# Centred gate sums as two rounded products, and a second pass that begins eight steps later, in a two-layer attention kernel

## The chip, the cores and the metric

The kernel runs on one core of one Trainium2 chip. The metric is the device time of one execution in microseconds (us), the median over several runs. Beside it stands one profiled execution, from which every row of a view is taken.

## The reference

Two layers over 2048 latent tokens and 256 context tokens, model width 1024. The even layer has two groups of heads side by side: softmax attention with latent projections, and gated linear attention in both directions (4 heads, key width 64, value width 128). The odd layer is a neighbourhood attention. The change touches the linear attention alone:

```python
def gla_inputs(gq, gk, gv, g_lr, gate_w, gate_b):
    ...
    logits = jnp.einsum('bnzr,zrk->bnzk', r, gate_w) + gate_b
    g = (jax.nn.log_sigmoid(logits.astype(jnp.float32)) / GATE_TAU).reshape(bsz, n, 2, B_HEADS, B_DK)
    return q, k, v, g[:, :, 0], g[:, :, 1]

def gla_scan(q, k, v, g, s0):
    ...
    def step(state, inp):
        qi, ki, vi, gi = inp
        b = jnp.cumsum(gi, axis=-2)
        b_last = b[..., -1:, :]
        q_t = qi * jnp.exp(b)
        k_t = ki * jnp.exp(-b)
        att = jnp.where(mask, jnp.einsum('bhld,bhmd->bhlm', q_t, k_t), 0.0)
        o = jnp.einsum('bhld,bhde->bhle', q_t, state) + jnp.einsum('bhlm,bhme->bhle', att, vi)
        k_dec = ki * jnp.exp(b_last - b)
        state = state * jnp.exp(b_last)[..., 0, :, None] + jnp.einsum('bhld,bhle->bhde', k_dec, vi)
        return state, o
    ...

def readout(a, b, za, zb):
    ...
    b = rms_norm(b, gla_gain).reshape(bsz, n, B_WIDTH).astype(zb.dtype) * jax.nn.silu(zb)
    return jnp.dot(jnp.concatenate([a, b], axis=-1), w_out)
```

## The kernel before, in words

The 2304 tokens are 18 tiles of 128. After the projections, `even_mix` runs the softmax attention (`even_attention`) and the linear attention (`gla`) at the same time. The program is written attention block by attention block, with the linear attention's code between them, and a scheduler of the framework sets each engine's order of instructions from a model of their times and from the order in which they are written. Places where the code asks that an instruction be issued after another (`issue_after`) bind it further.

The softmax attention goes through 4 pairs of heads, 5 query blocks each (one of the 256 context tokens, four of 512), and per block through its key tiles. A key tile has two score tiles `st`, one per head. Each is three products of rounded parts (high by high L1016, high by low L1017, low by high L1018), one exponential on ACT into `apt` (L106), and an accumulation on DVE (L1007); the value products (L958) follow some key tiles later, four key tiles at a time. Three PSUM banks hold score tiles, two hold the linear attention's results (`gl`). Counted over the whole attention there are 592 score tiles.

Products run on operands of full precision, which PE does in two records each, or on rounded operands (type `F32R`), one record each. A value split into a rounded part and the rounded remainder keeps nearly its whole precision; the kernel does that for its large matrix products.

The linear attention works on chunks of 128 tokens in three parts:

- First pass. `front(c)` makes the gate's logits (L728), their log-sigmoid through three ACT operations and one DVE operation (L734, tile `G`), and sums along the tokens, centred on the chunk's middle, as a product with a triangle `tri` of ones and minus ones: one product of 256 columns per direction (L739). Two exponentials of the result scale queries and keys. The first and last rows of `G` are written out (`gE`), since the scans need them. `back(c)` scales queries and keys (L761), transposes them (L768), makes the chunk's state increment (L773, L774), the products within the chunk for both directions (L782), their masks and the sum of both on DVE (L785, L787, tile `gat`), and the product with the values (L791). The chunks are staggered: a chunk's `back` is written between the steps of the next two chunks' `front`.
- Two scans over the 18 chunks, forward on GpSimd (POOL) and backward on DVE (`gsb`, L827 to L829).
- Second pass, one chunk at a time: `enter` adds the state's part (L848, L849) to what the first pass left, squares the sum on ACT and adds up the squares per head on DVE (L853), and takes the power on POOL; `leave` normalises, multiplies with the gate and transposes back. The results go to a buffer in memory, `RT`.

`even_attention` calls `hook` once per key tile, 296 times. From call 166 on every fourth call does one step of `later()`: six steps that load and split weights of the output projection, then the second pass, one chunk per step, with a further weight step in every second one, then the last weights. What is left of it when the last query block begins (call 278) is done there in one go. After the attention the output projection reads `RT`, its first two tiles' products being laid at the end of the attention.

Of the kernel before, what the change touches and what calls it, by code (L numbers as in the profile page):

```python
# [11 lines left out]
F32R = mybir.dt.float32r  # L12
AF = mybir.ActivationFunctionType
ALU = mybir.AluOpType
AX = mybir.AxisListType
PSUM = bass.MemoryType.PSUM

P = 128
# [70 lines left out]
class Kern:  # L89
# [600 lines left out]
    def gla(self, gp, gs, g1, gd, pp, tag):  # L690

        nc = self.nc
        g = nc.gpsimd
        H = 4
# [8 lines left out]
        nc.vector.tensor_tensor(out=gw[64:97], in0=raw[64:97], in1=gw[64:97], op=ALU.subtract)  # L703
        tri = self.tl(g1, [P, 4, P], "tri", bufs=1)
        nc.sync.dma_start(tri[:], self.i["tri"])
        gn = self.tl(gp, [P, 4], "gn")
        nc.sync.dma_start(gn[:], self.i["gla_norm"])
        g.tensor_scalar(out=gn[:], in0=gn[:], scalar1=0.5, scalar2=None, op0=ALU.mult)
# [6 lines left out]
        z4 = lambda a: a.rearrange("p (h z d) -> p h z d", z=2, h=H)  # L715

        def front(c):

            ps = bank()
            u3 = self.tl(gs, [P, 3, 32], "gu3")  # L720
            nc.sync.dma_start(u3[:], self.Un[c, :, 1024:1056].unsqueeze(1).to_broadcast([P, 3, 32]))
            nc.tensor.transpose(ps[:96, :P], u3[:].rearrange("p n d -> p (n d)"), self.ident[:])
            r = rT[c % 2]
            self.act(r[:96, :], ps[:96, :P])
            nc.vector.tensor_tensor(out=r[32:64, :], in0=ps[32:64, :P], in1=r[32:64, :], op=ALU.subtract)
            yield
            lg = bank()
            nc.tensor.matmul(lg[:], r[:], gw[:], start=True, stop=True)  # L728
            e = self.tl(gs, [P, 512], "ge")
            self.act(e[:], lg[:], AF.Abs)  # L730
            self.act(e[:], e[:], AF.Exp, scale=-1.0)
            self.act(e[:], e[:], AF.Ln, bias=1.0)
            G = self.tl(g1, [P, 512], "gG", bufs=1)
            nc.vector.scalar_tensor_tensor(out=G[:], in0=lg[:], scalar=0.0, in1=e[:], op0=ALU.min, op1=ALU.subtract)  # L734
            G4 = G[:].rearrange("p (h z d) -> p h z d", z=2, h=H)
            yield
            mid = bank()
            for z in range(2):
                nc.tensor.matmul(mid[:].rearrange("p (h z d) -> p h z d", z=2, h=H)[:, :, z, :], tri[:, z, :], G4[:, :, z, :], start=True, stop=True)  # L739
            nc.sync.dma_start(self.gE[c, :, 2], G[0::127])  # L740
            qt = self.tl(g1, [P, 512], "gqt", bufs=1)
            kt = self.tl(g1, [P, 512], "gkt", bufs=1)
            self.act(qt[:], mid[:], AF.Exp, scale=1 / 16)
            for z, t in enumerate((127, 0)):
                nc.sync.dma_start(self.gE[c, z : z + 1, 0], qt[t : t + 1])
            self.act(kt[:], mid[:], AF.Exp, scale=-1 / 16)
            nc.sync.dma_start(self.gE[c, :, 1], kt[0::127])
            tiles[c] = qt, kt
            yield
# [55 lines left out]

        tiles, inputs = {}, {}
        fr = [front(c) for c in range(NT)] + [iter(())] * 2
        fetch_u(0)
        for c in (0, 0, 1, 0, 1):
# [34 lines left out]
        def enter(c, qT, oi, zb):  # L844

            ps = bank()
            for h in range(H):
                nc.tensor.matmul(ps[:, h * P : h * P + P], qT[:, h, :], Dl[c][:, h, :], start=True, stop=True)  # L848
            nc.vector.tensor_tensor(out=oi[:], in0=ps[:], in1=oi[:], op=ALU.add)  # L849
            sq = self.tl(gs, [P, 512], "ge")  # L850
            self.act(sq[:], oi[:], AF.Square)
            ss = self.tl(gs, [P, H], "gss")
            nc.vector.tensor_reduce(out=ss[:], in_=sq[:].rearrange("p (h t) -> p h t", h=H), axis=AX.X, op=ALU.add)  # L853
            self.rpow(ss[:], ss[:], 1.0 / 128, EPS)
            return c, oi, zb, ss

# [13 lines left out]
        def second():  # L870

            order = self.back_order()
            old, cur = None, fetch(order[0])
            for c in order[1:] + [None, None]:
                if old:
                    leave(*old)
                old = enter(*cur) if cur else None
                cur = fetch(c) if c is not None else None
                yield
# [166 lines left out]
    def even_mix(self, e1, win, hT):  # L1046
        nc = self.nc
        self.RT = self.scr("RT", (KD, P, T), F32)
        self.x1 = self.scr("x1", (T, D), F32)
        with ExitStack() as es:  # L1050
            with ExitStack() as esa:
# [4 lines left out]
                g1 = self.pool(es, "glA", bufs=2, side="right", reuse_waits="tile")  # L1056
                esg = ExitStack()
                gp = self.pool(esg, "glC", side="right", reuse_waits="tile")
                gs = self.pool(esg, "glS", bufs=2, side="right", reuse_waits="tile")
                count, ld, w = [0], [], {}  # L1060

                def hook(mm, ex):

                    count[0] += 1
                    if count[0] >= 166 and count[0] % 4 == 2:
                        with self.tc.issue_after(mm.ins), self.tc.issue_after(ex.ins), self.tc.issue_after(self.add.ins):
                            next(slow, None)

# [22 lines left out]
                def later():  # L1091
# [11 lines left out]
                    for _ in ws:  # L1103
                        yield

                att = self.even_attention(ap, pp, hook)
                next(att)
                second, slow = self.gla(gp, gs, g1, gd, pp, "gl"), later()
# [773 lines left out]
```

## Time and profile before

| | us |
|---|---|
| median of 3 runs | 3619.09 |
| lowest and highest | 3616.67, 3619.68 |
| the profiled execution | 3617.2 |
| its span, from first to last instruction | 3615.4 |

The profile has a row per instruction of the engines PE (matrix products), PEld (their weight loads), DVE, ACT and POOL. The page sums up busy times; further views group them by line and shape, by stretch of time, or list who waited for whom. In a row of groups stand the count after an x, then the busy time in us, the mean duration in ns, and the idle time before with what ended it; in a row of waits the total in us, the number of times and the longest; in the timeline the start, the duration and the instruction, with the idle time in brackets. Since products are pipelined, PE's durations overlap: how long one takes is read from the distance of the starts. The times of the stages, by the first and last start of their lines: the softmax attention from 1085.1 to 1927.0 us, the centred sums from 1122.0 to 1543.5 us, the second pass's products with the state from 1646.9 to 1834.3 us.

### The profile page before, as it was taken

What the parts mean: (1) busy time and instruction counts of PE and PEld (TensorE: products, weight loads), DVE (VectorE), ACT (ScalarE), POOL (GpSimd) and SP (SyncE); (2) the same over time, 40 slices, a digit from 0 to 9 for tenths busy, and PEclk for the clock granted to TensorE, in tenths of its full rate; (3) what the DMA queues carried; (4) which work ended last, traced back from release to release, by engine and by line L of the source; (5) the groups of instructions that cost most, each with busy time, mean ns of one, the idle gap of its engine ahead of it and who ended that gap; (6) DMA issues with size and microseconds to landing.
All of it is one profiled execution on the core that took longest, in us unless ns stands there. A gap on an engine that the chain in (4) does not pass through costs nothing. (4 is left out here: it accounts for less than half of the span.)

```text
span 3615.4 us, 51630 instructions
## 1 busy us (share of the span) xinstructions
PE 3523.6 (97%) x18260; PEld 2734.3 (76%) x18260; DVE 2372.3 (66%) x4876; ACT 1430.5 (40%) x2705; POOL 1212.6 (34%) x1342
## 2 busy tenths in 40 slices
PE   8999999999999999999999999999999999999899
PEld 6988998888886666656667878888788886555577
DVE  4677665888886776787664345444587874667721
ACT  5544551111115555555653134444422223555510
POOL 1433430111011232212312233333334444677743
PEclk9999999999999999999999999999999999999999
DMA  7555463222233343334534544456643437888654
GB/s 253 149 153 159 141 191 99 87 77 84 75 109 89 83 104 83 94 92 129 163 91 143 162 164 127 145 143 199 212 139 123 139 122 202 213 213 222 185 178 146
DMA packets 396683, 513.62 MB, mean 142 GB/s; under 512 B 61229, under 2 KB 275197, under 8 KB 390522
## 3 DMA queue, kind: packets, MB, share of 16 engines
q1 hardware_dynamic: 353242, 418.68, 40.0%
q0 software_dynamic: 20192, 56.97, 5.6%
q10 hardware_dynamic: 22992, 34.68, 2.8%
q8 instruction: 145, 2.38, 0.3%
q14 instruction: 112, 0.92, 0.1%
HBM read 330.61 MB, written 179.59 MB: 141 GB/s over the span
## 5 line engine op out<-in xcount | busy, mean ns | idle before, releaser
L1007 DVE TENSOR_TENSOR acc<-acc,apt 128x512 f32<-128x512 f32 x512 | 376.4, 764 | 150.6 <-ACT apt L106 147.0
L666 DVE TENSOR_REDUCE mm<-mx 128x1 f32<-128x512 f32 (+1 forms) x656 | 392.7, 627 | 90.6 <-PE mx L665 82.3
L106 ACT ACTIVATE apt<-st 128x512 f32<-128x512 f32 (+1 forms) x592 | 342.9, 593 | 269.0 <-PE st L1018 229.5
L958 PE MATMUL av<-apt,av 128*64 128x512 f32 (+1 forms) x1184 | 269.2, 592 | 0.0
L1016 PE MATMUL st<-aq,akh 97*128 97x512 f32 x576 | 246.8, 428 | 0.2 <-ACT apt L106 0.2
L665 PE MATMUL mx<-mk,mq 96*128 96x512 f32 (+1 forms) x656 | 238.5, 372 | 0.0
L1017 PE MATMUL st<-aq,akh 96*128 96x512 f32 x576 | 229.1, 398 | 0.0
L1018 PE MATMUL st<-aq,akl 96*128 96x512 f32 x576 | 228.5, 397 | 0.0
L1450 DVE CUSTOM_DVE_ANT_1 mx<-mx,mtab 128x465 f32<-128x465 f32 (+14 forms) x576 | 183.9, 338 | 47.2 <-PE mx L1444 34.5
L106 ACT ACTIVATE u<-gm 128x352 f32<-128x352 f32 (+1 forms) x144 | 70.3, 495 | 358.5 <-PE gm L131 207.7
L106 ACT ACTIVATE opt<-opt 128x930 f32<-128x930 f32 (+9 forms) x144 | 119.2, 830 | 234.5 <-POOL opt L1748 137.0
L958 PEld LDWEIGHTS av<-apt,av 128*64 128x64 f32 x1184 | 79.9, 137 | 152.0 <-issue 150.0
L1708 DVE TENSOR_TENSOR opt<-st,tab 128x64 f32<-128x64 f32 (+10 forms) x576 | 143.0, 314 | 78.3 <-PE st L1548 44.7
L1583 POOL TENSOR_TENSOR oacc<-oacc,opt 128x682 f32<-128x682 f32 (+9 forms) x144 | 173.9, 1230 | 37.8 <-ACT opt L106 36.6
L1016 PEld LDWEIGHTS st<-aq,akh 97*128 97x128 f32 x576 | 109.0, 189 | 72.7 <-issue 44.2
L665 PEld LDWEIGHTS mx<-mk,mq 96*128 96x128 f32 x656 | 122.7, 188 | 11.7
L1018 PEld LDWEIGHTS st<-aq,akl 96*128 96x128 f32 x576 | 110.2, 191 | 25.5
L1017 PEld LDWEIGHTS st<-aq,akh 96*128 96x128 f32 x576 | 110.6, 192 | 17.8
L106 ACT ACTIVATE x<-px,modB,modA 128x128 f32<-128x128 f32 x272 | 99.1, 468 | 58.5 <-PE px L335 39.5
L1547 PE MATMUL st<-q,kt 128*128 128x480 f32 (+5 forms) x256 | 98.7, 388 | 20.2 <-DVE opt L1708 14.8
L129 PE MATMUL gm<-w0h,hhi 128*128 128x512 f32 x288 | 115.3, 400 | 2.3 <-DVE hhi L347 2.3
L129 PE MATMUL gm<-w1h,hhi 128*128 128x512 f32 x288 | 116.7, 405 | 0.0
(584 smaller groups left out, 9906.5 us busy)
## 6 DMA issues: line engine op xcount, KB each, us to landing
q<-Q SPq DMA_DIRECT2D x48, 512.0 KB
H<-x ACTq DMA_DIRECT2D x36, 512.0 KB
adaw<-ada_w SPq DMA_DIRECT2D x64, 256.0 KB
x<-H SPq DMA_DIRECT2D x32, 512.0 KB
K1t<-okt POOLq DMA_DIRECT2D x32, 512.0 KB, 6.7
kt<-K1t SPq DMA_DIRECT2D x32, 512.0 KB
mtab<-rpb_q SPq DMA_DIRECT2D x16, 899.0 KB
QT<-qkhl SPq DMA_DIRECT2D x36, 384.0 KB
```

Source lines behind the costliest of these rows:

```text
L106: return self.nc.scalar.activation(out, in_, func, **kw)
L129: self.nc.tensor.matmul(out, lh(k), rh(k), start=j == 0, stop=False)
L665: mm = nc.tensor.matmul(ps[:, :w], q[:A_QK, (t % 6) * P : (t % 6) * P + P], k[:A_QK, k0 : k0 + w], start=True, stop=True)
L666: nc.vector.tensor_reduce(out=m[:, t, n : n + 1], in_=ps[:, :w], axis=AX.X, op=ALU.max)
L958: nc.tensor.matmul(O[j, nb][i * 64 : i * 64 + 64, :w], V[j, kt // TT][:, kt % TT, i * 64 : i * 64 + 64], pts[i][:, :w], start=n == 0, stop ...
L1007: self.add = nc.vector.tensor_tensor(out=acc[i][:, :w], in0=a[:, :w], in1=pts[i][:, :w], op=ALU.add)
L1016: nc.tensor.matmul(ps[:, :w], kh[: A_QK + 1, i, kq], qh[: A_QK + 1, :w], start=True, stop=False)
L1017: nc.tensor.matmul(ps[:, :w], kh[:A_QK, i, kq], ql[:A_QK, :w], start=False, stop=False)
L1018: mm = nc.tensor.matmul(ps[:, :w], kl[:A_QK, i, kq], qh[:A_QK, :w], start=False, stop=True)
L1450: nc.vector.tensor_tensor_reduce(out=s, in0=s, in1=tb[:, ri : ri + rn, ci : ci + cn], scale=1.0, scalar=-3e38, op0=ALU.add, op1=ALU.max, a ...
L1583: self.psum = nc.gpsimd.tensor_tensor(out=a, in0=a, in1=pts[:, :, a0 - r0 : a1 - r0, :], op=ALU.add)
L1708: nc.vector.tensor_tensor(out=pt[:, d[0], d[1]], in0=ps[:, d[0], d[1]], in1=tabs[j][i][:, ri : ri + rn, ci : ci + cn], op=ALU.add)
```

## The change

The centred sums' product with full-precision operands becomes two with rounded ones. The log-sigmoid stays in the tile `e`; ACT copies it, rounding, into `G`; DVE makes the remainder `L` (in a further buffer of the small tiles `ge`); the triangle is rounded once into `trr`. Per direction PE then adds up the products of `trr` with `G` and with `L`. The rows for `gE` are now read from `e`. In the second pass the four heads' sums of squares are made by four DVE operations that multiply and add up in one, instead of an ACT square and a DVE sum. And `later()` begins at call 174 instead of 166.

```diff
+        trr = self.tl(gp, [P, 2, P], "trr", F32R, bufs=1)
+        self.act(trr[:], tri[:, :2, :])
...
-            G = self.tl(g1, [P, 512], "gG", bufs=1)
-            nc.vector.scalar_tensor_tensor(out=G[:], in0=lg[:], scalar=0.0, in1=e[:], op0=ALU.min, op1=ALU.subtract)
-            G4 = G[:].rearrange("p (h z d) -> p h z d", z=2, h=H)
+            nc.vector.scalar_tensor_tensor(out=e[:], in0=lg[:], scalar=0.0, in1=e[:], op0=ALU.min, op1=ALU.subtract)
+            nc.sync.dma_start(self.gE[c, :, 2], e[0::127])
+            G = self.tl(g1, [P, 512], "gG", F32R, bufs=1)
+            self.act(G[:], e[:])
+            L = self.tl(gs, [P, 512], "ge", F32R)
+            nc.vector.tensor_tensor(out=L[:], in0=e[:], in1=G[:], op=ALU.subtract)
+            G4, L4 = z4(G[:]), z4(L[:])
             yield
             mid = bank()
             for z in range(2):
-                nc.tensor.matmul(mid[:].rearrange("p (h z d) -> p h z d", z=2, h=H)[:, :, z, :], tri[:, z, :], G4[:, :, z, :], start=True, stop=True)
-            nc.sync.dma_start(self.gE[c, :, 2], G[0::127])
+                nc.tensor.matmul(z4(mid[:])[:, :, z, :], trr[:, z, :], G4[:, :, z, :], start=True, stop=False)
+                nc.tensor.matmul(z4(mid[:])[:, :, z, :], trr[:, z, :], L4[:, :, z, :], start=False, stop=True)
...
             sq = self.tl(gs, [P, 512], "ge")
-            self.act(sq[:], oi[:], AF.Square)
             ss = self.tl(gs, [P, H], "gss")
-            nc.vector.tensor_reduce(out=ss[:], in_=sq[:].rearrange("p (h t) -> p h t", h=H), axis=AX.X, op=ALU.add)
+            for h in range(H):
+                o = slice(h * P, h * P + P)
+                nc.vector.tensor_tensor_reduce(out=sq[:, o], in0=oi[:, o], in1=oi[:, o], scale=1.0, scalar=0.0,
+                                               op0=ALU.mult, op1=ALU.add, accum_out=ss[:, h : h + 1])
...
-                    if count[0] >= 166 and count[0] % 4 == 2:
+                    if count[0] >= 174 and count[0] % 4 == 2:
```

Line numbers of the changed kernel are higher by up to eight (L1016 is L1024, L791 is L797, L785 is L791 there). Each engine's order moves over the whole attention. Three places show how.

PE, the centred sums of the tenth chunk. Before (`st` score tiles, `av` value products, `gl` the linear attention's results):

```order
L958 MATMUL av_13576<-apt_13603,av_13417 64x512
L958 MATMUL av_13576<-apt_13609,av_13417 64x512
L739 MATMUL gl_11298<-gG_11251,tri_10547 128x4x64 x2
L782 MATMUL gl_11312<-gqT_11271,gkT_11272 128x128
L1016 MATMUL st_13649<-aq_13452,akh_1874_10509 128x512
L1017 MATMUL st_13649<-aq_13452,akh_1874_10509 128x512
```

and in the change:

```order
L1026 MATMUL st_13783<-aq_13544,akl_13507 128x512
L745 MATMUL gl_11349<-gG_11300,trr_10549 128x4x64
L746 MATMUL gl_11349<-ge_11302,trr_10549 128x4x64
L745 MATMUL gl_11349<-gG_11300,trr_10549 128x4x64
L746 MATMUL gl_11349<-ge_11302,trr_10549 128x4x64
L1024 MATMUL st_13789<-aq_13544,akh_1875_10510 128x512
```

Two products have become four, and they stand between other instructions of the attention than before.

PE, ahead of the tenth chunk's product with its values. Before, where four score tiles and six value products stand between the products within the chunk and the first row shown, and the product with the values (L791) follows the last one:

```order
L958 MATMUL av_13841<-apt_13799,av_12798 64x512
L958 MATMUL av_13841<-apt_13805,av_12798 64x512
L728 MATMUL gl_11403<-gw_10543,rT_1891_10553 128x512
L1016 MATMUL st_13846<-aq_13777,akh_1877_10512 128x512
L1017 MATMUL st_13846<-aq_13777,akh_1877_10512 128x512
L1018 MATMUL st_13846<-aq_13777,akl_13218 128x512
L1016 MATMUL st_13852<-aq_13777,akh_1877_10512 128x512
L1017 MATMUL st_13852<-aq_13777,akh_1877_10512 128x512
L1018 MATMUL st_13852<-aq_13777,akl_13218 128x512
L1016 MATMUL st_13860<-aq_13777,akh_1877_10512 128x512
L1017 MATMUL st_13860<-aq_13777,akh_1877_10512 128x512
L1018 MATMUL st_13860<-aq_13777,akl_13218 128x512
```

and in the change, where the first row shown ends the first score tile behind the products within the chunk:

```order
L1026 MATMUL st_13952<-aq_13869,akl_13310 128x512
L1024 MATMUL st_13958<-aq_13869,akh_1877_10512 128x512
L1025 MATMUL st_13958<-aq_13869,akh_1877_10512 128x512
L1026 MATMUL st_13958<-aq_13869,akl_13310 128x512
L1024 MATMUL st_13966<-aq_13869,akh_1874_10509 128x512
L1025 MATMUL st_13966<-aq_13869,akh_1874_10509 128x512
L1026 MATMUL st_13966<-aq_13869,akl_13405 128x512
L730 MATMUL gl_11460<-gw_10543,rT_1892_10555 128x512
L1024 MATMUL st_13972<-aq_13869,akh_1874_10509 128x512
L1025 MATMUL st_13972<-aq_13869,akh_1874_10509 128x512
L1026 MATMUL st_13972<-aq_13869,akl_13405 128x512
L797 MATMUL gl_11472<-gu_11316,gat_11445 128x128 x4
```

Seven score tiles, eight value products and the gate product ahead of the product with the values have become four score tiles and the gate product. So it is in the ninth to fourteenth chunk and in the sixteenth.

DVE, the masks (`ge`, `gat`) of the last chunk among the steps of the backward scan (`gsb`, `D`) and the normalisation of an attention block (`den`, `rc`). Before:

```order
L894 TENSOR_TENSOR den_14886<-den_14886,rc_14890 128x256
L828 TENSOR_TENSOR gsb_12096<-gsb_12096,D_1908_10572 64x512
L895 SCALAR_TENSOR_TENSOR rc_14890<-den_14886,rc_14890 128x256
L829 TENSOR_TENSOR D_1908_10572<-gsb_12092,fac_1926_10590 64x512
L896 TENSOR_TENSOR rc_14890<-av_14818,rc_14890 128x256
L785 TENSOR_TENSOR ge_11988<-gl_11990,tri_10547 128x512
L827 TENSOR_TENSOR gsb_12100<-gsb_12096,fac_1925_10589 64x512
L785 TENSOR_TENSOR gat_11987<-gl_11989,tri_10547 128x512
L828 TENSOR_TENSOR gsb_12100<-gsb_12100,D_1907_10571 64x512
L787 TENSOR_TENSOR gat_11987<-gat_11987,ge_11988 128x512
```

and in the change:

```order
L1015 TENSOR_TENSOR acc_3034_14841<-acc_3034_14841,apt_15022 128x512
L834 TENSOR_TENSOR gsb_12184<-gsb_12184,D_1910_10575 64x512
L1015 TENSOR_TENSOR acc_3033_14840<-acc_3033_14840,apt_15030 128x512
L1015 TENSOR_TENSOR acc_3034_14841<-acc_3034_14841,apt_15036 128x512
L835 TENSOR_TENSOR D_1910_10575<-gsb_12180,fac_1928_10593 64x512
L791 TENSOR_TENSOR ge_12080<-gl_12082,tri_10547 128x512
L791 TENSOR_TENSOR gat_12079<-gl_12081,tri_10547 128x512
L833 TENSOR_TENSOR gsb_12188<-gsb_12184,fac_1927_10592 64x512
L1015 TENSOR_TENSOR acc_3033_14840<-acc_3033_14840,apt_15044 128x512
L1015 TENSOR_TENSOR acc_3034_14841<-acc_3034_14841,apt_15050 128x512
L793 TENSOR_TENSOR gat_12079<-gat_12079,ge_12080 128x512
```

The normalisation and two scan steps no longer stand ahead of and between the masks; two accumulations stand behind them. On PE, four value products and four score tiles stood before between the last of these chunk's products and the one that needs `gat`; in the change eight and five.

## The prediction

> **What bounds the kernel now.** I read the page's totals first, then the busy time by stretch around the changed code, then who waited for whom there, then the timeline of the changed products.
>
> ```profile
> span 3615.4 us, 51630 instructions
> PE 3523.6 (97%) x18260; PEld 2734.3 (76%) x18260; DVE 2372.3 (66%) x4876; ACT 1430.5 (40%) x2705; POOL 1212.6 (34%) x1342
> ```
>
> ```profile
> core 0: us, PE busy (x) PEld busy (x) DVE busy (x) ACT busy (x) POOL busy (x), PEclk, DMA share, GB/s
> 1120.00:1550.00 430.00, 426.25 (x2197) 271.19 (x2197) 305.63 (x425) 243.55 (x468) 108.88 (x109) 1.00 0.36 90
> 1550.00:1645.00 95.00, 92.00 (x422) 54.84 (x420) 90.71 (x134) 50.99 (x88) 11.01 (x9) 1.00 0.25 73
> 1645.00:1840.00 195.00, 195.00 (x956) 122.97 (x954) 137.69 (x217) 117.73 (x249) 59.25 (x58) 1.00 0.53 148
> ```
>
> PE is busy 97% of the span. The three stretches are the first pass of the linear attention, its two scans, and its second pass, all laid between the products of the softmax attention. PE has work in all three, at a granted clock of 1.00; DVE is 71% busy in the first, 95% in the second and 71% in the third, ACT 57%, 54% and 60%. A busy row can hide stalls, so I look at PE's waits from 1120 to 1928 us:
>
> ```profile
> PE gl L791 <- DVE gat L787: 3.0, 1, 3.0
> PE gl L782 <- DVE rT L725: 2.2, 3, 0.7
> PE den L889 <- DVE rc L895: 0.7, 1, 0.7
> PE gl L768 <- DVE gG L734: 0.6, 1, 0.6
> PE st L1016 <- ACT apt L106: 0.2, 1, 0.2
> ```
>
> They come to 6.7 us in 808 us. So here a PE microsecond removed is a microsecond gained, and DVE or ACT time added costs nothing until it makes PE wait.
>
> **The centred sums.** Each of 18 chunks does two full-precision products with the triangle, 256 columns each. One chunk's pair between attention products, from PE's timeline:
>
> ```profile
> 1365.97 0.40 PE L1018 MATMUL st<-aq,akl 96*128 96x512 f32 x1
> 1366.21 1.03 PE L739 MATMUL gl<-gG,tri 128*128 128x256 f32 x4
> 1366.88 0.58 PE L1016 MATMUL st<-aq,akh 97*128 97x512 f32 x1
> 1367.30 0.40 PE L1017 MATMUL st<-aq,akh 96*128 96x512 f32 x1
> 1367.54 0.40 PE L1018 MATMUL st<-aq,akl 96*128 96x512 f32 x1
> ```
>
> The durations overlap; the starts count. Rounded products of 512 columns follow one another every 0.235 us. From the start of L739 to that of L1017 are 1.09 us; less one such step for L1016, the pair costs 0.86 us, or 0.215 for each of its four records. What a rounded product of 256 columns costs is seen in the later neighbourhood attention, on PE and on PE's weight loads:
>
> ```profile
> 2700.05 0.40 PE L129 MATMUL gm<-w0h,hhi 128*128 128x512 f32 x1
> 2700.28 0.40 PE L1437 MATMUL mx<-mk,mz 128*128 128x256 f32 x2
> 2700.52 0.39 PE L130 MATMUL gm<-w0l,hhi 128*128 128x512 f32 x1
> 2700.05 0.42 PEld L1437 LDWEIGHTS mx<-mk,mz 128*128 128x128 f32 x2
> ```
>
> Two of them take 0.24 us start to start, 0.12 each, each with a weight load of its own. Four per chunk are 0.48. Saved: 0.86 - 0.48 = 0.38 us a chunk, times 18 = **6.9 us**, all on the path that sets the end. The bounds are 0.12 and today's 0.215 a product (nothing saved); I take 0.12, the row of the same width, kind and full weight load.
>
> [...]
>
> **What the first pass pays for it** is an ACT copy (rounding) and a DVE subtraction per chunk. Means by shape:
>
> ```profile
> L1007 DVE TENSOR_TENSOR acc<-acc,apt 128x512 f32<-128x512 f32 x512 | 376.4, 764 | 150.6 <-ACT apt L106 147.0
> L787 DVE TENSOR_TENSOR gat<-gat,ge 128x512 f32<-128x512 f32 x18 | 14.8, 823 | 0.0
> L785 DVE TENSOR_TENSOR ge<-gl,tri 128x512 f32<-128x512 f32 x18 | 12.4, 689 | 0.5
> L853 DVE TENSOR_REDUCE gss<-ge 128x4 f32<-128x512 f32 x18 | 12.2, 679 | 1.0 <-ACT ge L106 0.9
> L106 ACT ACTIVATE D<-wraw 128x512 fp32r<-128x512 f32 x9 | 5.6, 622 | 0.0
> L106 ACT ACTIVATE ge<-goi 128x512 f32<-128x512 f32 x18 | 11.2, 621 | 0.0
> ```
>
> The copy is like the split of a weight, 0.62 us; the subtraction lies between 0.69 and 0.82. That is 11 us more for ACT and at most 15 for DVE over 430 us in which they idle 186 and 124: counted as nothing. The order shows why the chain itself is covered: between the score tile of the last exponential ahead of the copy and the second product PE has at least five score tiles, 5 x 3 x 0.235 = 3.5 us, and in all but one chunk also eight or more value products. Behind the waiting copy on ACT stand the exponentials that free PE's three score banks; that is the last rival. The boundary rows now leave by DMA from the unrounded tile; on SP that DMA keeps its place, between the writes of a chunk's own outputs and of its queries, so nothing new waits there. The one rounding of the triangle stands behind the gate weights' rounding and before the first products: nothing.
>
> **The order around it** moves by more than that. The last chunk held PE for the 3.0 us shown above. DVE's timeline, and PE's product that waited:
>
> ```profile
> 1569.09 0.68 DVE L785 TENSOR_TENSOR ge<-gl,tri 128x512 f32<-128x512 f32 x1
> 1569.80 0.74 DVE L827 TENSOR_TENSOR gsb<-gsb,fac 64x512 f32<-64x512 f32 x1
> 1570.57 0.69 DVE L785 TENSOR_TENSOR gat<-gl,tri 128x512 f32<-128x512 f32 x1
> 1571.29 0.69 DVE L828 TENSOR_TENSOR gsb<-gsb,D 64x512 f32<-64x512 f32 x1
> 1572.01 0.69 DVE L787 TENSOR_TENSOR gat<-gat,ge 128x512 f32<-128x512 f32 x1
> 1564.91 1.94 PE L958 MATMUL av<-apt,av 128*64 128x512 f32 x8
> 1566.77 0.50 PE L1016 MATMUL st<-aq,akh 97*128 97x512 f32 x1
> 1572.85 0.57 PE L791 MATMUL gl<-gu,gat 128*128 128x128 f32 x3 [3.00 <-DVE gat L787]
> ```
>
> The masks were late because DVE had scan steps and a normalisation ahead of and between them. Eight value records, four products, took 1.86 us. Before, PE had four value products and four score tiles (4 x 0.705) ahead of the waiting product, 4.7 us; now eight and five, 7.2 us. Were DVE as late as before, the wait would fall from 3.0 to 0.5: **2.5 us gained** (bounds 0 and 3.0).
>
> In seven other chunks (the ninth to fourteenth and the sixteenth) the order now leaves PE only four score tiles and the gate product, 4 x 0.705 + 0.235 = 3.05 us, where DVE must do two masks and their sum, 0.69 + 0.69 + 0.82 = 2.2 us. The 0.85 between them must hold the hand-overs and what DVE still has in hand. I charge 0.15 each, **1.0 us lost**; the bounds are nothing and one accumulation late each, 7 x 0.76 = 5.3.
>
> **The second pass.** ACT loses its square (0.62), DVE its sum (0.68), for four multiply-and-sum operations of 128 elements, each with a read of its sum. The nearest are the masked maxima of 124 elements, whose start-to-start distances are 0.25 and 0.38 us:
>
> ```profile
> 2705.95 0.33 DVE L1450 CUSTOM_DVE_ANT_1 mx<-mx,mtab 128x124 f32<-128x124 f32 x1
> 2706.20 0.26 DVE L1450 CUSTOM_DVE_ANT_1 mx<-mx,mtab 128x56 f32<-128x56 f32 x1
> 2708.35 0.30 DVE L1450 CUSTOM_DVE_ANT_1 mx<-mx,mtab 128x124 f32<-128x124 f32 x1
> 2708.73 0.39 DVE L1450 CUSTOM_DVE_ANT_1 mx<-mx,mtab 128x217 f32<-128x217 f32 x1
> ```
>
> Four cost 1.0 to 1.5 us, 0.3 to 0.8 more than the sum did: 6 to 15 us of DVE over a stretch of 195 us in which it idles 57. Nothing reaches PE. L787 and L1007, with both inputs in SBUF, are slower on average (0.82, 0.76) than L785, which reads PSUM (0.69). [...]
>
> The eight steps' delay moves the second pass, its DMAs on SP and the six first weight splits by 16 score tiles. In the order its last transpose stands at tile 543 of 592 instead of 527, so 49 tiles remain; the last weights are still split, and the first output tiles still loaded, before the attention's last products. The same PE work lies elsewhere between the same attention products: nothing, unless its cover, attention still to run, were gone. Beyond the stage the order differs only in a few exchanged products: nothing.
>
> **The sum** is made against the profiled execution, 3617.2 us (span 3615.4 and 1.8 around it): -6.9 - 2.5 + 1.0 = -8.4, so 3608.8. The median of the three runs is 3619.1, 1.9 higher; from it the same change gives **3610.7 us**. A measurement of this kernel tells about 0.2% (7.2 us) from no change, so the line lies at 3611.9 and the forecast only just beyond it.
>
> **Rivals.** *The narrow places.* DVE is one accumulation late at each of the seven, +5.3, and the last chunk still waits: 3619.1 - 6.9 + 5.3 = 3617.5; with the last chunk relieved 3615. For it: DVE is 71% busy, its accumulations take 0.76 where 0.69 is possible. Against: PE waited for that operation once in 18 chunks. Chance 0.15, no change.
>
> *Short products don't hide their weight loads,* or the strided columns, or the second product, aren't done at 0.12 us, so that the change doesn't do what it says. The loads of the triangle today:
>
> ```profile
> L739 PEld LDWEIGHTS gl<-gG,tri x72: 187/188/193, 1121.8 to 1543.3; 128*128 128x128 f32 x72
> L739 PE MATMUL gl<-gG,tri x72: 377/378/483, 1122.0 to 1543.5; 128*128 128x256 f32 x72
> ```
>
> The number of loads stays at 72. If each product lasts its load's 0.19 us, the saving is (0.86 - 0.76) x 18 = 1.8; at 0.215 it is 0. With -2.5 and +1.0 the time is 3615.8 to 3617.6. Against: the L1437 pair. Chance 0.09, no change.
>
> *Slower: the rounding copy holds up ACT.* It waits for the log-sigmoid on DVE, with up to three exponentials between in the order, none in one chunk. If DVE starts it three accumulations late, 3 x 0.69 = 2.07, and takes 0.69 for it, ACT stands 2.76 us; PE's two free score banks cover 2 x 0.705 = 1.41; 1.35 is lost, times 18 = 24 us: 3619.1 - 6.9 + 24 = 3636. It decides from 1.41 + 14.1/18 = 2.2 us of standing on, where it outweighs the gain by 7.2. For it: the new hand-over goes ACT, DVE, ACT, DVE. Against: PE waited for ACT's exponentials 0.2 us in all. Chance 0.10.
>
> **How the numbers follow.** The forecast has 0.66: by the bounds of its terms 0.54 lies below 3611.9 and 0.12 above. With the two middle rivals, 0.15 + 0.09, no change has 0.36; slower has 0.10. The low end takes the whole 3.0 us wait and the other 3.7 us of PE's waits as gone: 3619.1 - 6.9 - 3.0 - 3.7 = 3605.5. The high end, 3619, takes in both middle rivals. Left out are the slower case and a little below.
>
> **What would show it.** Right: two rounded rows in place of L739's, together 72 records at steps of 0.12 us; PE's wait for the last masked sum under 1 us; DVE higher in the second pass with PE's waits unchanged. Wrong: steps of 0.19 or more at the new products; PE waiting for the masked sums in the later chunks; score products waiting for exponentials while ACT stands at the rounding copy.

## The result, and the profile after

The changed kernel takes 3612.4 us (median of 14 runs, 3606.4 to 3617.5); the kernel before, run beside it on the same chip, 3620.1 us. The ratio is 0.9981, with a 95% interval from 0.9973 to 0.9989: faster by 0.11 to 0.27%. The profiled execution's span went from 3615.4 to 3608.2 us, by 7.2.

After's page totals, then its busy times in the same three stretches:

```profile
span 3608.2 us, 51577 instructions
PE 3515.8 (97%) x18260; PEld 2726.7 (76%) x18260; DVE 2394.8 (66%) x5020; ACT 1431.6 (40%) x2706; POOL 1210.2 (34%) x1342
...
1120.00:1550.00 430.00, 425.29 (x2212) 269.86 (x2211) 321.60 (x447) 252.03 (x489) 108.69 (x112) 1.00 0.37 90
1550.00:1645.00 95.00, 94.51 (x426) 55.55 (x427) 87.81 (x128) 49.16 (x85) 8.03 (x6) 1.00 0.25 70
1645.00:1840.00 195.00, 195.00 (x949) 122.25 (x949) 144.84 (x337) 112.78 (x231) 57.42 (x55) 1.00 0.55 151
```

PE is as full as before and its number of records is the same; DVE has 16.0 us more in the first stretch (third busy column, 321.6 against 305.6) and 7.2 more in the third. PE's busy time is 1.0 us lower in the first (425.3 against 426.3) and the same in the third. What PE waited for from 1120 to 1928 us:

```profile
PE gl L797 <- DVE gat L793: 3.0, 6, 0.9
PE den L897 <- DVE rc L903: 1.4, 1, 1.4
PE gl L730 <- DVE ge L791: 0.4, 1, 0.4
PE st L1024 <- ACT apt L106: 0.4, 2, 0.2
```

They are 5.2 us instead of 6.7. The wait for the masked sum (L797 for `gat`) has the same 3.0 us as before, but in six pieces instead of one. PE's timeline shows the four new products of one chunk, and the last chunk's product with the values:

```profile
1318.64 0.28 PE L745 MATMUL gl<-gG,trr 128*128 128x256 f32 x1
1318.76 0.28 PE L746 MATMUL gl<-ge,trr 128*128 128x256 f32 x1
1318.88 0.28 PE L745 MATMUL gl<-gG,trr 128*128 128x256 f32 x1
1318.99 0.28 PE L746 MATMUL gl<-ge,trr 128*128 128x256 f32 x1
1319.11 0.40 PE L1024 MATMUL st<-aq,akh 97*128 97x512 f32 x1
...
1573.95 1.13 PE L797 MATMUL gl<-gu,gat 128*128 128x128 f32 x8 [0.29 <-DVE gat L793]
```

Four starts at distances of 0.12 us, 0.47 us for the chunk. Where the last chunk had PE stand for 3.0 us, it now stands for 0.29. Added up over the softmax attention, from each PE start to the next, the triangle's records take 15.1 us before and 9.4 after; that is 5.7 of the gain, and the waits are 1.5. The attention's time from its first score product to the start of its last value product went from 841.9 us (1085.1 to 1927.0) to 835.7 (1084.1 to 1919.7), by 6.3. Not all of that belongs to the change. Behind a wait of 1.9 us at the attention's beginning, ahead of the first changed product, the granted clock (the column ahead of the last two) was lower in the profiled execution of before, whose row comes first:

```profile
1080.00:1100.00 20.00, 17.78 (x72) 12.51 (x71) 7.49 (x13) 8.69 (x16) 6.68 (x8) 0.83 0.74 184
1080.00:1100.00 20.00, 17.77 (x79) 12.44 (x78) 8.94 (x16) 10.68 (x20) 6.69 (x8) 0.91 0.76 190
```

Over 20 us that is 3.4 us of clock lost before and 1.8 after: 1.6 of the 6.3.

### The profile page after: what moved, and what is told of

Read it like the earlier page. It is cut to its first block, busy times and chain, and to the rows that moved or that the text cites. A ratio compares the mean times of both kernels' runs of the same rounds, so it can differ in the third digit from the quotient of the medians.

```text
span 3608.2 us, 51577 instructions
## 1 busy us (share of the span) xinstructions
PE 3515.8 (97%) x18260; PEld 2726.7 (76%) x18260; DVE 2394.8 (66%) x5020; ACT 1431.6 (40%) x2706; POOL 1210.2 (34%) x1342
## 4 chain that ended last, share of the span: by engine, by line
PE 69%; issue 15%; DVE 6%; DMA 5%; POOL 3%; ACT 2%; SPq 0%; POOLq 0%; DVEq 0%; ACTq 0%
PE gm L131 7%; PE gm L129 7%; PE gm L130 7%; PE av L966 6%; PE st L1024 4%; PE st L1025 3%; PE st L1026 3%; PE o L1585 2%; PE st L1555 2%; PE st L129 2%; PE st L131 2%; PE st L130 2%; PE o L1567 2%; PE st L1556 2%; PE pj L131 1%
## 5 line engine op out<-in xcount | busy, mean ns | idle before, releaser
L1024 PE MATMUL st<-aq,akh 97*128 97x512 f32 x576 | 245.5, 426 | 0.4 <-ACT apt L106 0.4
L1024 PEld LDWEIGHTS st<-aq,akh 97*128 97x128 f32 x576 | 108.6, 189 | 70.5 <-issue 44.6
L665 PEld LDWEIGHTS mx<-mk,mq 96*128 96x128 f32 x656 | 122.8, 188 | 11.7
L1025 PEld LDWEIGHTS st<-aq,akh 96*128 96x128 f32 x576 | 110.3, 192 | 17.3
```

The lines of the kernel that those rows point to most:

```text
L665: mm = nc.tensor.matmul(ps[:, :w], q[:A_QK, (t % 6) * P : (t % 6) * P + P], k[:A_QK, k0 : k0 + w], start=True, stop=True)
L1024: nc.tensor.matmul(ps[:, :w], kh[: A_QK + 1, i, kq], qh[: A_QK + 1, :w], start=True, stop=False)
L1025: nc.tensor.matmul(ps[:, :w], kh[:A_QK, i, kq], ql[:A_QK, :w], start=False, stop=False)
```

## The experiments

The change has three parts that can be separated: the rounded products (with their copy, subtraction and early boundary rows), the sums of squares on DVE, and the delay. Every kernel below ran in five rounds beside the kernel before on the same chip.

| kernel | products | sums | begins at call | median, us | ratio to before | 95% interval |
|---|---|---|---|---|---|---|
| `whole` | yes | yes | 174 | 3611.97 | 0.9974 | 0.9965 to 0.9983 |
| `products_only` | yes | no | 166 | 3620.53 | 0.9996 | 0.9987 to 1.0004 |
| `delay_only` | no | no | 174 | 3621.09 | 1.0003 | 0.9993 to 1.0013 |
| `sums_only` | no | yes | 166 | 3619.61 | 0.9996 | 0.9986 to 1.0006 |
| `products_sums` | yes | yes | 166 | 3617.20 | 0.9989 | 0.9979 to 0.9999 |
| `products_delay` | yes | no | 174 | 3612.81 | 0.9980 | 0.9969 to 0.9991 |
| `delay_sums` | no | yes | 174 | 3619.91 | 0.9998 | 0.9988 to 1.0008 |
| `product_dose` | yes, 8 more | yes | 174 | 3627.51 | 1.0017 | 1.0009 to 1.0026 |
| `before_early` | no | no | 162 | 3627.11 | 1.0025 | 1.0016 to 1.0034 |
| `whole_170` | yes | yes | 170 | 3612.78 | 0.9977 | 0.9968 to 0.9986 |
| `whole_182` | yes | yes | 182 | 3610.62 | 0.9972 | 0.9963 to 0.9982 |
| `one_product` | one of two | yes | 174 | 3615.85 | 0.9989 | 0.9980 to 0.9998 |

**Each part alone, and the whole again.** `products_only` is the change with these two parts put back:

```diff
-            for h in range(H):
-                o = slice(h * P, h * P + P)
-                nc.vector.tensor_tensor_reduce(out=sq[:, o], in0=oi[:, o], in1=oi[:, o], ...)
+            self.act(sq[:], oi[:], AF.Square)
+            nc.vector.tensor_reduce(out=ss[:], in_=sq[:].rearrange("p (h t) -> p h t", h=H), axis=AX.X, op=ALU.add)
...
-                    if count[0] >= 174 and count[0] % 4 == 2:
+                    if count[0] >= 166 and count[0] % 4 == 2:
```

> The rounded products alone: the second pass begins at call 166 as before and has the ACT square and the DVE sum as before. By the theory that PE's products are the gain, 7 to 8 us under the kernel before (6.9 from the products, up to 1.5 from PE's waits), as much as the whole change. By the rival that the delayed second pass or the shorter ACT list brings it, 0 to 2 us under. The first pass's order on PE is that of the whole change, so the same waits for the masked sums are expected, about 3 us.

`delay_only` is the kernel before with `174`, `sums_only` the kernel before with the four DVE operations, `whole` the change itself.

> The eight steps' delay alone. By the theory, no change: within 2 us of the kernel before, since the same PE work lies elsewhere between the same attention products; the 3.0 us wait for the last chunk's masks stays, as it lies ahead of the second pass. By the rival that the delay is the gain, 5 us or more under.

> The sums of squares on DVE alone. By the theory, no change: within 2 us of the kernel before; DVE's busy time in the second pass up by 6 to 15 us. By the rival that DVE reaches PE there, 5 us or more over.

> The whole change again, on the same chip as its parts. 7 to 8 us under the kernel before; by the theory equal to the products alone within 2 us, and the three parts' differences add up to it within 3 us.

By their times `delay_only`, `sums_only` and `whole` came out as expected (DVE's added time in `sums_only` was 4.8 us from 1645 to 1840, below the 6 to 15). `products_only` did not: the only part that takes work from PE gained nothing by itself, though its own steps are there in its trace. So the whole change isn't the sum of its parts, which `whole` was expected to be. Where the products' gain went is seen at the beginning of the second pass. First the kernel before, from the timelines of DVE and PE (the last step of DVE's backward scan, PE's first product with the state, DVE's addition of it):

```profile
1640.58 0.69 DVE L829 TENSOR_TENSOR D<-gsb,fac 64x512 f32<-64x512 f32 x1
...
1646.86 1.16 PE L848 MATMUL gl<-D,gqT 128*128 128x128 f32 x8
...
1648.06 0.69 DVE L849 TENSOR_TENSOR goi<-gl,goi 128x512 f32<-128x512 f32 x1 [0.65 <-PE gl L848]
```

The scan's last step starts 6.3 us before PE's product, and DVE waits for PE. Now the same in `products_only`, with ACT and PE behind it:

```profile
1640.68 1.16 PE L854 MATMUL gl<-D,gqT 128*128 128x128 f32 x8
...
1647.00 0.69 DVE L835 TENSOR_TENSOR D<-gsb,fac 64x512 f32<-64x512 f32 x1
1647.72 0.69 DVE L855 TENSOR_TENSOR goi<-gl,goi 128x512 f32<-128x512 f32 x1
...
1648.44 0.63 ACT L106 ACTIVATE ge<-goi 128x512 f32<-128x512 f32 x1 [5.27 <-DVE goi L855]
...
1649.61 0.80 PE L1022 MATMUL st<-aq,akh 97*128 97x512 f32 x1 [4.97 <-ACT apt L106]
1650.20 0.63 PE L1023 MATMUL st<-aq,akh 96*128 96x512 f32 x1
```

PE got to the second pass earlier, DVE to the end of its scan later, and the order of the two is turned round: the product stands 6.3 us ahead of the scan's last step. DVE adds the state's part 7 us after the product began. ACT's square waits 5.27 us for it, the exponentials stand behind the square, PE runs out of score banks and waits 4.97 us. Even then the loss isn't over. `products_only`'s busy times in stretches of 10 us (the column ahead of the last two is the granted clock):

```profile
1640.00:1650.00 10.00, 5.03 (x25) 3.48 (x22) 9.62 (x16) 2.16 (x5) 0.12 (x1) 0.94 0.17 48
1650.00:1660.00 10.00, 10.00 (x26) 4.98 (x27) 6.48 (x11) 4.66 (x9) 3.08 (x3) 0.55 0.05 8
```

Behind the wait the clock was 0.94 and 0.55: PE is busy all through the second row, but its score products start 0.43 us apart instead of 0.235. That is 0.6 + 4.5 = 5.1 us of clock lost, of which 0.4 still fell into the wait (an estimate: at a clock of 0.50, which the trace of before shows from 1087 to 1093 us, the 0.6 us lost by 1650 put its fall at 1648.8; PE began at 1649.6). Wait and clock together take some 10 us, more than the products and the last chunk's relief had brought: the attention's time is 846.0 us (1084.5 to 1930.5), 4.1 above the kernel before. So the theory that "the products gain wherever they stand" fell. Two remained: that the square on ACT is the culprit, which either other part would remove (A), or that the second pass must not begin before DVE's scan is over (B).

**Pairs.** `products_sums` is the change with `166`; `products_delay` is the change with the square and the sum of before; `delay_sums` is the kernel before with the other two parts.

> The rounded products and the sums of squares on DVE, with the second pass beginning at call 166 as before. Theory A (in the products alone a square on ACT waited 5 us for DVE's scan, the exponentials stood behind it, PE waited 5.0 us and lost about 5 us more at half clock; either other part takes that wait away, here because ACT has no square to wait with): the gain is there, 6 to 9 us below the kernel before (3611 to 3614), ratio 0.9975 to 0.9983, and no wait of PE for apt over 1 us near 1650 us. Theory B (what matters is only that DVE has done with the backward scan when the second pass begins): without the delay nothing is gained, ratio 0.999 to 1.001, and PE waits some 3 to 5 us near 1650 us for something of DVE.

> The rounded products and the second pass eight steps later, the square staying on ACT. Theory A: the scan is done when the first square is due, so ACT doesn't wait with the exponentials behind it: 6 to 9 us below the kernel before, ratio 0.9975 to 0.9983. Theory B says the same here. Rival C (the square on ACT itself is what costs, wherever the second pass begins): PE waits for ACT again by 3 to 5 us, ratio 0.999 to 1.000.

> The two other parts without the rounded products. Theories A and B: both are cover alone and gain nothing; ratio 0.9990 to 1.0005, PE keeps the one wait of 3.0 us for the last chunk's masks. Rival D (delay and sums together gain by themselves, and the products only little): ratio 0.9975 to 0.9985.

`delay_sums` gains nothing, so rival D falls. `products_delay` has the whole gain, with the square on ACT as before, and PE waits 0.2 us for ACT, so rival C falls too. Its timelines have the order of the kernel before again, with a larger distance:

```profile
1646.79 0.69 DVE L835 TENSOR_TENSOR D<-gsb,fac 64x512 f32<-64x512 f32 x1
...
1663.27 1.16 PE L854 MATMUL gl<-D,gqT 128*128 128x128 f32 x8
```

`products_sums` lies between what A and B said: 0.9989, some 4 us gained instead of 6 to 9 or none. Its trace is B's in a milder form:

```profile
1642.88 1.16 PE L854 MATMUL gl<-D,gqT 128*128 128x128 f32 x8
...
1649.50 0.69 DVE L835 TENSOR_TENSOR D<-gsb,fac 64x512 f32<-64x512 f32 x1
...
1651.80 4.90 DVE L1015 TENSOR_TENSOR acc<-acc,apt 128x512 f32<-128x512 f32 x8
1656.62 0.68 DVE L868 TENSOR_TENSOR goi<-goi,gss 128x512 f32<-128x512 f32 x1
...
1657.43 1.26 POOL L869 TENSOR_TENSOR goi<-goi,gsf 128x512 f32<-128x512 f32 x1 [3.44 <-DVE goi L868]
...
1658.75 0.66 PE L872 MATMUL gl<-ident,goi 128*128 128x128 f32 x4 [2.37 <-POOL goi L869]
```

The scan is late by 6.6 us here too. With no square, ACT has nothing to wait with, but the backlog is still there: eight accumulations come first on DVE, then the normalisation, POOL's multiplication, and the transposes on PE, which wait 2.37 us. In the stretch behind it the clock fell again:

```profile
1655.00:1660.00 5.00, 2.63 (x16) 2.02 (x16) 4.93 (x9) 2.35 (x6) 1.83 (x2) 0.97 0.09 10
1660.00:1665.00 5.00, 5.00 (x18) 4.05 (x18) 5.00 (x14) 2.65 (x7) 1.66 (x2) 0.69 0.70 204
```

0.15 + 1.55 = 1.7 us. So A isn't the full cause: without the square there is still a wait and a lower clock behind the late scan. The sums on DVE soften the loss without the delay: by the two traces, wait and clock take 4.1 us instead of some 10. The times alone don't decide this, since the interval of `products_sums` (0.9979 to 0.9999) reaches into both forecasts and overlaps those of `products_only` and of `products_delay`. What they do tell apart is `products_only` (0.9987 to 1.0004) and the whole change (0.9965 to 0.9983).

**The same collision in the kernel before.** If B is right, the products aren't needed for the loss.

```diff
-                    if count[0] >= 166 and count[0] % 4 == 2:
+                    if count[0] >= 162 and count[0] % 4 == 2:
```

> The kernel before with one edit: the second pass begins at call 162 instead of 166, one step earlier. In the kernel before, DVE's last scan step begins at 1640.6 us and PE's first product of the second pass with the state at 1646.9. Theory B' (what cost the rounded products their gain is that the second pass runs into DVE's backward scan): one step is some 11 to 13 us, so that product now comes 5 to 7 us ahead of the scan's end, as in the products alone; ACT's square waits for DVE, PE waits 3 to 6 us once near 1645 to 1655 us, and half a clock behind it can cost some us more: 3 to 9 us slower than before, ratio 1.0008 to 1.0025. Rival E (the loss comes with the rounded products themselves, for instance their ACT copies): no change, ratio 0.9995 to 1.0005, and no such wait.

3627.1 us, a ratio of 1.0025 (1.0016 to 1.0034): slower by as much as B' allowed, and the change's rounded products aren't in it. Its timelines, and the stretch of 10 us:

```profile
1636.82 1.16 PE L848 MATMUL gl<-D,gqT 128*128 128x128 f32 x8
...
1640.44 0.69 DVE L829 TENSOR_TENSOR D<-gsb,fac 64x512 f32<-64x512 f32 x1
...
1642.49 0.63 ACT L106 ACTIVATE ge<-goi 128x512 f32<-128x512 f32 x1 [3.18 <-DVE goi L849]
...
1643.66 0.80 PE L1016 MATMUL st<-aq,akh 97*128 97x512 f32 x1 [2.88 <-ACT apt L106]
```

```profile
1640.00:1650.00 10.00, 7.12 (x20) 4.45 (x20) 6.58 (x11) 4.64 (x9) 1.71 (x2) 0.68 0.00 1
1650.00:1660.00 10.00, 10.00 (x51) 6.59 (x48) 6.04 (x10) 5.36 (x13) 1.45 (x2) 0.98 0.34 100
```

The product is 3.6 us ahead of the scan's end, ACT's square waits, PE waits 2.88 us and loses 3.2 + 0.2 = 3.4 more at the lower clock. Rival E is refuted.

**How much delay.** `whole_170` and `whole_182` are the change with these numbers in place of 174.

> The whole change with the second pass at call 170, one step later than before instead of two. By theory B' its first product with the state comes some 5 us behind the end of DVE's scan, so half the delay is enough: as the whole change, ratio to the kernel before 0.9972 to 0.9984, no wait of PE over 2 us near 1650 us. Rival F (both steps of delay are needed): a wait of 2 to 5 us there, ratio 0.9985 to 0.9995.

> The whole change with the second pass at call 182, two steps later still. By theory B' no wait is left to remove at its beginning: as the whole change, ratio 0.9972 to 0.9984. If the stage's end has no room for two more steps (the whole change leaves 49 score tiles behind the last transpose, this one some 33, so it should): 0.9985 or more, with PE waits behind 1900 us.

Both came out by B'; the wait of 2 to 5 us that rival F asked for isn't in the trace of `whole_170`. The time of `whole_182` is the lowest measured, but `whole`, `whole_170`, `whole_182` and the change itself can't be told apart. In `whole_170` the distance is 5.1 us:

```profile
1646.04 0.69 DVE L835 TENSOR_TENSOR D<-gsb,fac 64x512 f32<-64x512 f32 x1
...
1651.12 1.16 PE L854 MATMUL gl<-D,gqT 128*128 128x128 f32 x8
```

So the sign of the distance from the scan's last step to the first product separates the kernels. It is negative in `products_sums` (-6.6 us), `products_only` (-6.3) and `before_early` (-3.6), and in these PE waits 2.4 to 5.0 us there; in the other eleven it is +5.1 us or more, and PE has no such wait. The size doesn't order them: -3.6 cost more than -6.6.

**Is PE the bound, and do weight loads show?** `product_dose` repeats the first product four times in each direction; the real ones overwrite what it makes.

```diff
             for z in range(2):
+                for _ in range(4):
+                    nc.tensor.matmul(z4(mid[:])[:, :, z, :], trr[:, z, :], G4[:, :, z, :], start=True, stop=True)
                 nc.tensor.matmul(z4(mid[:])[:, :, z, :], trr[:, z, :], G4[:, :, z, :], start=True, stop=False)
```

> The whole change with eight more rounded products of 0.12 us in each of the 18 chunks, overwritten by the real ones: 144 of them, 17.3 us of PE work. If PE is the bound of the stage throughout: 17.3 us above the whole change, less 2 to 3 us of waits in the narrow places that the longer group of products would cover, so 14 to 18 us above it (3626 to 3630), ratio to the kernel before 1.0015 to 1.0028. If the weight loads showed between the products (0.19 to 0.215 us each): 27 to 31 us above. If PE had slack there: under 10 us above.

It is 15.5 us above `whole` (3627.5 - 3612.0); by the ratios, 1.0017 and 0.9974, it is 0.0043 or 15.6 us, and their intervals leave some 4.6 to both sides. That agrees with a stage bound by PE at 0.12 us a product (17.3); the 27 to 31 of visible loads are excluded. It isn't a clean dose, though. The order moved, and a new wait came, which the expectation didn't have (ACT's timeline, then PE's):

```profile
1548.47 0.20 ACT L106 ACTIVATE fac<-fac 128x4 f32<-128x4 f32 x1 [9.16 <-DMA fac<-gE]
...
1549.21 0.50 PE L1026 MATMUL st<-aq,akh 97*128 97x512 f32 x1 [3.31 <-ACT apt L106]
```

An ACT operation of 0.20 us stood 9.16 us waiting for a DMA, with the exponentials behind it. Its waits from 1120 to 1928 us are 4.3 us all the same, against 5.7 in `whole`, since of the waits for masked sums only the last chunk's is left (0.4); a clock of 0.91 from 1540 to 1560 us cost 1.8. By these terms it should stand 17.3 - 1.4 + 1.8 = 17.7 above `whole`. In the two profiled executions the attention took 848.1 and 836.4 us, only 11.7 more. From start to start the triangle's records do take 17.6 more (27.0 against 9.4), so other steps of PE took some 6 us less, and why stays open. The dose shows the price of a product, and that most of it reaches the time, but not that all of it does.

**One product less.** `one_product` leaves the remainder out (product L746 and subtraction L740).

```diff
-            L = self.tl(gs, [P, 512], "ge", F32R)
-            nc.vector.tensor_tensor(out=L[:], in0=e[:], in1=G[:], op=ALU.subtract)
...
-                nc.tensor.matmul(z4(mid[:])[:, :, z, :], trr[:, z, :], L4[:, :, z, :], start=False, stop=True)
```

> The whole change without the remainder: its product and its subtraction on DVE are left out, so the centred sums are those of the rounded operand alone. 36 products of 0.12 us less, 4.3 us of PE work, and 18 DVE operations of 0.69 us less. If PE is the bound throughout, 3 to 5 us below the whole change (some of it lost again, since the narrow places get narrower by 0.24 us): ratio to the kernel before 0.9960 to 0.9975. If DVE or the narrow places had become the bound, the 12 us less of DVE would bring more, 6 us and over: 0.9955 or less.

A miss: 0.9989, outside the 0.9960 to 0.9975 that was expected. By the medians it is some 3 to 5 us slower than the whole change (0.9981 and 0.9974 in its two measurements) instead of 4 faster; the intervals overlap. Its PE timeline and the stretch behind it:

```profile
1564.23 2.04 PE L794 MATMUL gl<-gu,gat 128*128 128x128 f32 x8 [3.49 <-DVE gat L790]
```

```profile
1560.00:1570.00 10.00, 6.51 (x22) 5.19 (x21) 9.62 (x15) 2.99 (x5) 0.00 (x0) 0.66 0.37 121
1570.00:1580.00 10.00, 10.00 (x44) 5.89 (x42) 8.38 (x13) 5.24 (x9) 0.00 (x0) 1.00 0.08 25
```

With 18 DVE operations fewer the scheduler went back to an order in which the last chunk's masks stand among the scan's steps. The wait that the change had removed is back, 3.49 us, and the clock of 0.66 is 3.4 us of clock lost, of which by estimate (a clock of 0.50 up to 1570, so from 1563.2 us on) 0.5 fell into the wait: some 6 us in the profiled execution, against 4.3 saved. Its attention took 837.4 us, against 835.7 and 836.4 in the two profiles of the whole change. So this run says nothing on the price of a product; it shows that the relief of the last chunk can be worth as much as that product.

## Why the prediction was right, and where it wasn't

The time (3610.7 forecast, 3612.4 measured), its sign and its range held. Point by point:

- **The products**: the mechanism held as worked out, 0.12 us a product, with the loads hidden: after's 72 loads of the triangle take 0.19 us each, under products that start 0.12 us apart. By the starts the triangle's records fell by 5.7 us, not 6.9 (0.38 times 18 is itself 6.8): in the whole stage they took 15.1 before (0.84 a chunk instead of 0.86) and 9.4 after (0.52 instead of 0.48).
- **The last chunk**: 2.5 us forecast, 2.7 measured (3.0 to 0.29), and for the reason given: from the start of the chunk's products (1563.8 and 1565.0 us) to the end of the masked sum (1572.7 and 1573.8) DVE took 8.9 us before and 8.8 after, so it was as late as before and PE had more to do meanwhile. The wait's real cost is more variable: in `delay_only` and `sums_only`, where this wait stays, a clock of 0.83 and 0.67 over the next 10 us cost 1.7 and 3.3 us more; in the profiled execution of before it cost nothing more. A row of `sums_only` and the same stretch of before:

```profile
1570.00:1580.00 10.00, 6.99 (x23) 5.60 (x22) 9.66 (x15) 3.29 (x7) 0.73 (x1) 0.67 0.31 96
```

```profile
1570.00:1580.00 10.00, 7.15 (x36) 4.15 (x36) 9.66 (x15) 3.47 (x6) 0.00 (x0) 1.00 0.35 118
```

- **The narrow places**: 1.0 us forecast for seven chunks, and 1.0 is what PE waited at these seven (0.2 at the ninth and at the twelfth, 0.56 at the sixteenth, the others none). But it waited as well at the seventh chunk, 0.92 us, and at the fifteenth, 0.77, which the forecast hadn't named: 2.7 in all, and one of its signs of being wrong. The order had left PE much work there, so the term lacked that DVE can be late for another reason. The fifteenth's 0.77 us is in the last section. Ahead of the seventh chunk's masks DVE had to scale the eighth chunk's queries in place, and stood 4.45 us for a DMA that writes rows of them out (DVE's timeline, then PE's):

```profile
1303.78 0.69 DVE L767 TENSOR_TENSOR gqt<-gqt,gu 128x512 f32<-128x512 f32 x1 [4.45 <-DMA gE<-gqt]
...
1308.35 1.13 PE L797 MATMUL gl<-gu,gat 128*128 128x128 f32 x8 [0.92 <-DVE gat L793]
```

- **Work on ACT and DVE counted as nothing**: right for ACT's copy (PE waited 0.4 us for exponentials) and for the sums on DVE (four took 0.85 us, not 1.0 to 1.5). The slower rival, ACT held by the rounding copy, didn't happen in any kernel with that copy. For the subtraction it is open: with it DVE's last scan step starts at 1642.8 to 1649.5 us (the dose apart), in the five kernels without the products at 1636.4 to 1642.7, and in `one_product`, which has products without the subtraction but differs in its order too, at 1631.0.
- **The sum**: -5.7 for the products, -2.7 for the last chunk, +2.7 for the other masked sums, and -1.5 for the other waits of PE, which come and go with the order (2.2 for `rT` went, 0.7 more for `rc` came), make -7.2. That this is the span's 7.2 is luck. Of the attention's 6.3, 1.6 is the clock at its beginning, so 4.7 is left for the terms: PE's other steps took some 2.5 us more. About half of that, 1.2 by the starts, lies at the same masked sums, since a product's record of 0.40 us hides the first 0.17 of each pause behind it; the rest is open. The median over all runs fell by 7.7; part of that can be the lower clock behind the last chunk's wait, which cost four other kernels with that wait 0 to 3.4 us and the profiled execution of before nothing. The forecast's -8.4 took the products 1.2 too high, the last chunk 0.2 too low and the masked sums 1.7 too low, and didn't count the 1.5: errors that partly cancel.
- **The step that failed** is the one on the eight steps' delay: "The same PE work lies elsewhere between the same attention products: nothing, unless its cover, attention still to run, were gone." I looked for its cost at the end of the attention, where there is none, and not at its beginning. There it is worth the whole gain while the square stays on ACT: products without it gained nothing (0.9996), products with it 0.20% (0.9980), it alone nothing (1.0003). With the sums on DVE, products without it kept some of the gain (0.9989, interval to 0.9999). The trace of before had the rows for it: 6.3 us between the scan's last step and the second pass's first product, and I forecast that PE would gain 8.4 on a DVE that gains nothing. That is half of it: in `products_only` PE's product came 6.2 us earlier, and DVE's last step 6.4 us later. The forecast was right since the products came together with the delay; its term "all on the path that sets the end" was true only under that condition, which I didn't name, and that the change met it was luck as far as the forecast goes.

## What to carry to other kernels

When work is taken from the engine that is the bound, everything that it feeds by count or by position comes earlier, and what another engine does in parallel doesn't, or comes later if the change gives that engine work: look for the next meeting point of the two, and measure their distance before and after (here 6.3 us turned into -6.3). A part of a change that costs and gains nothing alone can be the condition for the gain of another; test pairs, not only single parts. And a waiting instruction is as dear as what stands behind it in its engine's order: a square of 0.63 us stood 5.27 us with the exponentials behind it, and PE, out of score banks, stood 4.97.

## What the runs showed of the hardware

**A wait of PE can cost more than its length.** In the fourteen traces of this case PE had ten single waits of 2.4 to 5.0 us between 1120 and 1928 us. Behind eight of them the granted clock fell, for a loss of 1.7 to 1.8 us (four times), 3.3 to 3.4 (three times, in `sums_only`, `before_early` and `one_product`) or 5.1 (`products_only`), which is one, two or three times the same piece (all of the lower clock is counted, also what fell into the wait itself); behind two of 3.0 and 3.1 us (before and `delay_sums`) it stayed at 1.00. The shortest of the eight were 2.37 us (`products_sums`) and 2.88 (`before_early`). In the traces of before and after no stretch of 10 us from 1120 to 1930 us shows less than 1.00, with waits of up to 1.4 us in them beside the 3.0 of before. At the attention's beginning, ahead of it, a wait of 1.9 us was followed by a lower clock in both: 0.50 for 6.8 us before (from 1086.5 us on) and for 3.4 us in the change (from 1086.1), two of these pieces and one. Why it stayed at 1.00 behind two of the long waits isn't shown by any run here.

**DVE beside POOL.** The fifteenth chunk's wait of after, from the timelines of DVE and POOL:

```profile
1499.65 2.60 DVE L1015 TENSOR_TENSOR acc<-acc,apt 128x512 f32<-128x512 f32 x1
1502.17 0.68 DVE L793 TENSOR_TENSOR gat<-gat,ge 128x512 f32<-128x512 f32 x1
...
1499.41 1.03 POOL L833 TENSOR_TENSOR gsf<-gsf,fac 64x512 f32<-64x512 f32 x1
1500.41 1.28 POOL L906 TENSOR_TENSOR rc<-rc,azt 128x512 f32<-128x512 f32 x1
```

One accumulation took 2.60 us instead of 0.69, and ended 0.56 us after the second of two POOL operations beside it. The masked sum behind it came late, and PE waited 0.77 us at 1502.99. In this trace 371 of the 512 accumulations had no POOL operation beside them and took 0.68 to 0.69 us; the other 141 took 1.00 on average, and all 58 that took over 0.8 us are among them. No run here took the POOL operations away, so it isn't shown that they are the cause.
